# Batched 64x64 matmul on one core: stores in 1 KB runs, output copied out by half partitions, and transposes of bf16 pairs

## The chip, the cores and the metric

The kernel runs on one core of one Trainium2 chip. The metric is the device time of one execution in microseconds (us). Runs are compared by their median; a profile shows one execution, with its own time.

## The reference

```python
def setup_inputs():
    return {
        "a": np.random.randn(1024, 64, 64).astype(np.float32),
        "b": np.random.randn(1024, 64, 64).astype(np.float32),
    }

def reference(a, b):
    return np.matmul(a, b).astype(np.float32)
```

There are 1024 independent products of 64x64 matrices. Each of a, b and the result holds 16.78 MB in fp32, so 33.55 MB are read and 16.78 MB written.

## The kernel before

**Tiles.** b and the result go in 16 tiles t of 64 batches (1 MB each), a in 8 tiles s of 128 batches (2 MB each), so one a tile serves two tiles t. A batch in a tile t is g*4 + h, with 16 groups g of four batches h. Four batches share one matmul: their 64 values of k are taken as 32 pairs (k = 2*kp + u), the contraction runs over the 128 partitions (h kp), and the two values of u are summed in PSUM. The stationary operand is block diagonal: rows of batch h meet only the 32 columns of batch h, and the rest stays at the zeros that two memsets put there at the start.

**The steps for a.** `load_a(s)` (L60) issues four DMAs of 512 KB on the POOL queue, one for each h, in runs of 4 KB, and casts to bf16 on the way. `regroup(s)` (L85) is one VectorE copy that puts the four h side by side, `a_bf`. `transpose(s, w)` (L92) makes 16 TensorE transposes of 128x128 bf16 (every second k, `u::2`, of one row of a per partition) into two PSUM tiles `at_ps`; VectorE copies one to `at_sb` and ScalarE the other, both with a reordering of the free dimensions. It is called for w = 0 and w = 1, so 32 transposes for an a tile. `spread(t)` (L107) is four VectorE copies inside SBUF, one for each h, of 32 partitions x 2048 bf16 elements: they put `at_sb` into the diagonal blocks of one of two tiles `at_bd`.

**The steps for b and the result.** `load_b(t)` (L70) is one DMA of 1 MB in runs of 512 B (two rows of k in one partition), on ScalarE's queue for t = 1 and 3 and on SyncE's (SP) queue otherwise. `cast(t)` (L117) is one ScalarE copy to bf16, or four quarters over both engines for the last tile. `multiply(t)` (L135) makes 64 pairs of weight load and matmul (16 g x 2 w x 2 u, 64 columns each) into four PSUM tiles `o_ps` of one bank, each of which ScalarE copies, 128 partitions x 512 elements, to `o_sb` (for the last tile, VectorE takes every second one). `store(t)` (L131) issues the DMA of 1 MB from `o_sb` on the POOL queue, in runs of 512 B: a partition (h mo) holds two rows of the result, w = 0 and 1, for each g. The last tile's store is issued in four quarters.

**Buffers.** Three a tiles, four b tiles, two each of `a_bf`, `at_sb`, `b_bf` and `at_bd`, five `o_sb`; in PSUM four `at_ps` and four `o_ps`, one bank each.

**The order.** It is written by hand (`tc.manual_schedule()`): each engine and each DMA queue takes its instructions in the order of the program text. For each t the text has `spread(t+1)`; for even t then `regroup(s+2)` and `load_a(s+4)`; `multiply(t)`; `cast(t+1)`; `load_b(t+4)`; a half of the transposes of a coming a tile; and `store(t-1)`. At the start `load_a(0)` comes first; the memset of the identity matrix stands behind its first DMA, and b(0) and b(1) carry an added dependency on that memset:

```python
            if s == 0 and h == 1:
                begun.append(nc.gpsimd.memset(identity[:], 0.0))
...
                reason="first load of a goes ahead",
```

Of the kernel before, what the change touches and what calls it, by code (L numbers as in the profile page):

```python
# [6 lines left out]

fp32 = mybir.dt.float32
bf16 = mybir.dt.bfloat16
# [3 lines left out]
def kernel(  # L13
# [9 lines left out]

    nc = tc.nc
    B, M, K = a.shape
    _, _, N = b.shape
# [2 lines left out]
    n_t, n_s = B // 64, B // 128  # L31
    A_AHEAD = 3
    B_AHEAD = 4
    N_BD = 2
# [1 line left out]

    a_v = a.rearrange("(s g h) (mp v) k -> s h g mp (v k)", h=4, g=32, v=16)
    b_v = b.rearrange("(t g h) (kp u) n -> t (h kp) g (u n)", h=4, g=16, u=2)
    o_v = out.rearrange("(t g h) (mo w) n -> t (h mo) g (w n)", h=4, g=16, w=2)

    consts = ctx.enter_context(tc.tile_pool(name="consts", bufs=1))
    a_pool = ctx.enter_context(tc.tile_pool(name="a_pool", bufs=A_AHEAD))
    b_pool = ctx.enter_context(tc.tile_pool(name="b_pool", bufs=B_AHEAD))
    work = ctx.enter_context(tc.tile_pool(name="work", bufs=2))
    o_pool = ctx.enter_context(tc.tile_pool(name="o_pool", bufs=5))
    t_psum = ctx.enter_context(
        tc.tile_pool(name="t_psum", bufs=4, space=bass.MemoryType.PSUM)
    )
    o_psum = ctx.enter_context(
        tc.tile_pool(name="o_psum", bufs=4, space=bass.MemoryType.PSUM)  # L50
    )

    bd_tiles = [
        consts.tile([128, 64, 4, 32], bf16, name=f"at_bd{i}") for i in range(N_BD)
    ]
    identity = consts.tile([128, 128], bf16)
    a_tiles, b_tiles, abf_tiles, at_tiles, bbf_tiles = {}, {}, {}, {}, {}
    held, begun = {}, []

    def load_a(s):  # L60
        a_sb = a_pool.tile([128, 4, 16, 64], bf16, name="a_sb")
        for h in range(4):
            if s == 0 and h == 1:
                begun.append(nc.gpsimd.memset(identity[:], 0.0))  # L64
            nc.gpsimd.dma_start(  # L65
                out=a_sb[:, h, :, :].rearrange("p v k -> p (v k)"), in_=a_v[s, h]
            )
        a_tiles[s] = a_sb

    def load_b(t):  # L70
        b_sb = b_pool.tile([128, 16, 128], fp32, name="b_sb")
        queue = nc.scalar if t in (1, 3) else nc.sync
        load = queue.dma_start(out=b_sb[:], in_=b_v[t])  # L73
        if t < 2:
            tc.add_manual_dep(
                load.ins,
                begun[0].ins.name,
                mybir.DependencyInfo(
                    mybir.DependencyClass.Sync, mybir.DependencyReason.DATA
                ),  # L80
                reason="first load of a goes ahead",
            )
        b_tiles[t] = b_sb

    def regroup(s):  # L85
        a_sb = a_tiles.pop(s)
        a_bf = work.tile([128, 16, 4, 64], bf16, name="a_bf")
        nc.vector.tensor_copy(a_bf[:], a_sb[:].rearrange("p h v k -> p v h k"))  # L88
        abf_tiles[s] = a_bf
        at_tiles[s] = work.tile([128, 2, 2, 128, 8], bf16, name="at_sb")  # L90

    def transpose(s, w):  # L92
        a_cols = abf_tiles[s][:].rearrange("p v h k -> p v (h k)")
        for u in range(2):
            at_ps = t_psum.tile([128, 8, 128], bf16, name="at_ps")
            for vo in range(8):
                nc.tensor.transpose(  # L97
                    at_ps[:, vo, :], a_cols[:, 2 * vo + w, u::2], identity[:]
                )
            dst = at_tiles[s][:, w, u, :, :]  # L100
            src = at_ps[:].rearrange("p vo q -> p q vo")
            if u == 0:
                nc.vector.tensor_copy(dst, src)  # L103
            else:
                nc.scalar.copy(dst, src)  # L105

    def spread(t):  # L107
        at_v = at_tiles[t // 2][:].rearrange(
            "p w u (g mp) vo -> p (w u) g (mp vo)", g=32
        )  # L110
        half = slice(16 * (t % 2), 16 * (t % 2) + 16)
        bd_v = bd_tiles[t % N_BD][:].rearrange("p (wu g) h mo -> p wu g h mo", g=16)
        for h in range(4):
            rows = slice(32 * h, 32 * h + 32)
            nc.vector.tensor_copy(bd_v[rows, :, :, h, :], at_v[rows, :, half, :])  # L115

    def cast(t):  # L117
        b_bf = work.tile([128, 16, 128], bf16, name="b_bf")
        b_sb = b_tiles.pop(t)
        if t < n_t - 1:  # L120
            nc.scalar.copy(b_bf[:], b_sb[:])  # L121
        else:
            for gq in range(4):
                rows = slice(4 * gq, 4 * gq + 4)
                if gq % 2:
                    nc.vector.tensor_copy(b_bf[:, rows, :], b_sb[:, rows, :])  # L126
                else:
                    nc.scalar.copy(b_bf[:, rows, :], b_sb[:, rows, :])  # L128
        bbf_tiles[t] = b_bf

    def store(t):  # L131
        for piece in held.pop(t):
            piece()

    def multiply(t):  # L135
        at_bd, b_bf = bd_tiles[t % N_BD], bbf_tiles.pop(t)
        last = t == n_t - 1
        o_sb = o_pool.tile([128, 4, 4, 2, 64], fp32, name="o_sb")

        def put(gq):  # L140
            nc.gpsimd.dma_start(  # L141
                out=o_v[t, :, 4 * gq : 4 * gq + 4, :],
                in_=o_sb[:, gq, :, :, :].rearrange("p g w n -> p (g w n)"),
            )

        def put_all():
            nc.gpsimd.dma_start(  # L147
                out=o_v[t], in_=o_sb[:].rearrange("p q g w n -> p (q g w n)")
            )

        for gq in range(4):
            o_ps = o_psum.tile([128, 4, 2, 64], fp32, name="o_ps")
            for g4 in range(4):
                g = 4 * gq + g4
                for w in range(2):
                    for u in range(2):
                        nc.tensor.matmul(  # L157
                            o_ps[:, g4, w, :],
                            at_bd[:, (2 * w + u) * 16 + g, :, :].rearrange(
                                "p h mo -> p (h mo)"  # L160
                            ),
                            b_bf[:, g, 64 * u : 64 * u + 64],
                            start=(u == 0),
                            stop=(u == 1),
                        )
            if last and gq % 2:
                nc.vector.tensor_copy(o_sb[:, gq, :, :, :], o_ps[:])  # L167
            else:
                nc.scalar.copy(o_sb[:, gq, :, :, :], o_ps[:])  # L169
        held[t] = [lambda q=q: put(q) for q in range(4)] if last else [put_all]  # L170

    with tc.manual_schedule():
        load_a(0)
        for t in range(B_AHEAD):
            load_b(t)
        for bd in bd_tiles:
            nc.vector.memset(bd[:], 0.0)  # L177
        nc.gpsimd.affine_select(  # L178
            out=identity[:],
            in_=identity[:],  # L180
            compare_op=mybir.AluOpType.not_equal,
            fill=1.0,
            base=0,
            pattern=[[-1, 128]],
            channel_multiplier=1,
        )
        for s in range(1, A_AHEAD):
            load_a(s)
        regroup(0)
        transpose(0, 0)  # L190
        transpose(0, 1)
        spread(0)
        cast(0)
        regroup(1)
        load_a(A_AHEAD)
        transpose(1, 0)
        for t in range(n_t):
            s, half = t // 2, t % 2
            if t + 1 < n_t:
                spread(t + 1)  # L200
            if half == 0:
                if s + 2 < n_s:
                    regroup(s + 2)
                if s + 1 + A_AHEAD < n_s:
                    load_a(s + 1 + A_AHEAD)
            multiply(t)
            if t + 1 < n_t:
                cast(t + 1)
            if t + B_AHEAD < n_t:
                load_b(t + B_AHEAD)  # L210
            if half == 0 and s + 1 < n_s:
                transpose(s + 1, 1)
            if half == 1 and s + 2 < n_s:
                transpose(s + 2, 0)
            if t >= HOLD - 1:
                store(t - HOLD + 1)
        for t in range(n_t - HOLD + 1, n_t):
            store(t)
# [30 lines left out]
```

## Time and profile before

| what | value |
|---|---|
| median of 5 runs (lowest to highest) | 139.31 us (138.28 to 139.67) |
| profiled execution, its own time | 139.6 us |
| its span (first to last instruction) | 137.7 us |
| HBM traffic over the span | 365 GB/s |
| busy: VectorE (DVE) | 84.9 us, 62% |
| busy: ScalarE (ACT) | 77.4 us, 56% |
| busy: TensorE matmul (PE), weight load (PEld) | 58.5 us, 56.5 us |
| busy: GpSimd (POOL), DMA issue included | 42.3 us, 31% |
| DMA queue 0 (POOL: a and the result), share of 16 engines | 66.2% |
| DMA queues 1 and 10 (SP and ScalarE: b), share of 16 engines | 30.1%, 3.9% |

How to read it: the span is what the profile covers, and the execution's time has 1.9 us around it. Engines run side by side, so busy times don't add up to the span. The 16 DMA engines serve all queues; their row in the profile's slices gives their mean busy share in tenths of a slice of 3.4 us, and the GB/s beside it counts the bytes written, so a cast from fp32 to bf16 counts half of what it reads. A group of instructions is one line of the kernel on one engine: its busy time, the mean time of one, and the idle time of the engine just ahead of them with what ended it. L12 is line 12 of the kernel before.

### The profile page before, as it was taken

To read this page: it belongs to the slowest core of one execution; us is meant where nothing else is said; L and a number is where in the kernel's file an instruction comes from. 1 tells how busy PE (TensorE), PEld (TensorE's weight loads), DVE (VectorE), ACT (ScalarE), POOL (GpSimd) and SP (SyncE) were. 2 spreads that over 40 slices of the span, in tenths; PEclk is the share of its full clock that TensorE was granted. 3 is DMA by queue.
4 is the path that set the end of the run, shared out by engine and by line. 5 is a ranking of instruction groups with operands and counts; after the bars stand their busy time and mean duration, and the time that the engine had idled before them with its cause. 6 is when DMAs were issued, how large, how long until landed. Compare 5 with 4: busy or idle time off the path is not lost.

```text
span 137.7 us, 2995 instructions
## 1 busy us (share of the span) xinstructions
PE 58.5 (42%) x1280; PEld 56.5 (41%) x1280; DVE 84.9 (62%) x94; ACT 77.4 (56%) x98; POOL 42.3 (31%) x57
## 2 busy tenths in 40 slices
PE   0000720595349745862065800857019645507100
PEld 0000720595249744761065800856019645507100
DVE  5771574681999899999339850699207867904200
ACT  0103171099917999960789209791297999715100
POOL 6921411332731612333113443430030330232600
PEclk9999996589965899999559995599955999995955
DMA  2999999999999999999999999999999999999980
GB/s 28 181 300 306 305 305 308 299 271 259 233 272 270 339 338 271 281 372 386 314 272 299 380 378 296 272 323 385 374 381 382 377 384 384 377 383 375 301 255 21
DMA packets 17469, 42.14 MB, mean 306 GB/s; under 512 B 1072, under 2 KB 1072, under 8 KB 17456
## 3 DMA queue, kind: packets, MB, share of 16 engines
q0 software_dynamic: 9008, 25.17, 66.2%
q1 hardware_dynamic: 7392, 14.68, 30.1%
q10 hardware_dynamic: 1056, 2.10, 3.9%
q8 instruction: 10, 0.16, 0.4%
q14 instruction: 3, 0.02, 0.0%
HBM read 33.55 MB, written 16.78 MB: 365 GB/s over the span
## 4 chain that ended last, share of the span: by engine, by line
DMA 57%; issue 25%; POOL 11%; POOLq 1%
DMA a_sb<-in_a_dram 40%; DMA out_dram<-o_sb 18%; POOL out_dram L147 6%; POOL a_sb L65 3%; POOL out_dram L141 2%; POOLq L244 1%; POOL identity L178 0%; POOL identity L64 0%; POOLq L147 0%; POOLq L178 0%; POOLq L141 0%; POOLq L65 0%; POOLq L233 0%
## 5 line engine op out<-in xcount | busy, mean ns | idle before, releaser
L157 PE MATMUL o_ps<-b_bf,at_bd 128*128 128x64 bf16 x1024 | 40.2, 208 | 46.7 <-ACT b_bf L121 38.8
L115 DVE COPY at_bd<-at_sb 32x2048 bf16<-32x2048 bf16 x64 | 46.9, 732 | 21.4 <-ACT at_sb L105 20.4
L157 PEld LDWEIGHTS <-at_bd 128*128 128x128 bf16 x1024 | 39.6, 108 | 48.2 <-issue 36.1
L169 ACT COPY o_sb<-o_ps 128x512 f32<-128x512 f32 x62 | 33.5, 615 | 25.8 <-DMA out_dram<-o_sb 17.0
L65 POOL DMA_DIRECT2D a_sb<-in_a_dram x32 | 20.1, 642 | 41.3 <-DMA a_sb<-in_a_dram 30.7
L147 POOL DMA_DIRECT2D out_dram<-o_sb x15 | 18.6, 1237 | 41.7 <-ACT o_sb L169 26.7
L97 PE MATMUL at_ps<-identity,a_bf 128*128 128x128 bf16 x256 | 20.5, 245 | 22.8 <-DVE a_bf L88 22.8
L121 ACT CAST b_bf<-b_sb 128x2048 bf16<-128x2048 f32 x15 | 29.1, 1943 | 0.0
L97 PEld LDWEIGHTS <-a_bf 128*128 128x128 bf16 x256 | 18.0, 112 | 23.2 <-DVE a_bf L88 23.2
L105 ACT COPY at_sb<-at_ps 128x1024 bf16<-128x1024 bf16 x16 | 16.8, 1048 | 11.7 <-PE at_ps L97 11.7
L103 DVE COPY at_sb<-at_ps 128x1024 bf16<-128x1024 bf16 x16 | 19.5, 1221 | 3.8 <-PE at_ps L97 3.5
L88 DVE COPY a_bf<-a_sb 128x4096 bf16<-128x4096 bf16 x8 | 10.0, 1250 | 10.2 <-DMA a_sb<-in_a_dram 10.1
L177 DVE MEMSET at_bd<- 128x4096 uint32 x2 | 6.9, 3472 | 2.5 <-PEq L233 1.7
L105 ACT ACT_TABLE_LOAD x1 | 1.3, 1283 | 6.9 <-issue 6.9
L141 POOL DMA_DIRECT2D out_dram<-o_sb x4 | 3.0, 754 | 4.4 <-ACT o_sb L169 4.1
L167 DVE COPY o_sb<-o_ps 128x512 f32<-128x512 f32 x2 | 1.4, 690 | 2.6 <-PE o_ps L157 2.6
L128 ACT CAST b_bf<-b_sb 128x512 bf16<-128x512 f32 x2 | 1.1, 616 | 3.1 <-DMA b_sb<-in_b_dram 3.1
L126 DVE CAST b_bf<-b_sb 128x512 bf16<-128x512 f32 x2 | 0.8, 424 | 3.4 <-DMA b_sb<-in_b_dram 3.4
L73 ACT MOVE_SHAPE b_sb<-in_b_dram x2 | 0.6, 320 | 3.2 <-POOL identity L64 2.2
L178 POOL TENSOR_SCALAR_AFFINE_SELECT identity<-identity 128x128 bf16<-128x128 bf16 x1 | 0.4, 354 | 0.0
L64 POOL MEMSET identity<- 128x128 bf16 x1 | 0.2, 224 | 0.0
L233 POOL MEMSET const-float32-0.0<- 128x1 f32 x1 | 0.1, 99 | 0.2 <-issue 0.2
(3 smaller groups left out, 0.3 us busy)
## 6 DMA issues: line engine op xcount, KB each, us to landing
out_dram<-o_sb POOLq DMA_DIRECT2D x15, 1024.0 KB, 21.2
a_sb<-in_a_dram POOLq DMA_DIRECT2D x32, 256.0 KB, 18.0
out_dram<-o_sb POOLq DMA_DIRECT2D x4, 256.0 KB, 7.6
b_sb<-in_b_dram SPq DMA_DIRECT2D x14, 0.5 KB, 21.1
b_sb<-in_b_dram ACTq DMA_DIRECT2D x2, 0.5 KB, 22.0
```

The source lines that it names most:

```text
L65: nc.gpsimd.dma_start(out=a_sb[:, h, :, :].rearrange("p v k -> p (v k)"), in_=a_v[s, h])
L88: nc.vector.tensor_copy(a_bf[:], a_sb[:].rearrange("p h v k -> p v h k"))
L97: nc.tensor.transpose(at_ps[:, vo, :], a_cols[:, 2 * vo + w, u::2], identity[:])
L103: nc.vector.tensor_copy(dst, src)
L105: nc.scalar.copy(dst, src)
L115: nc.vector.tensor_copy(bd_v[rows, :, :, h, :], at_v[rows, :, half, :])
L121: nc.scalar.copy(b_bf[:], b_sb[:])
L141: nc.gpsimd.dma_start(out=o_v[t, :, 4 * gq : 4 * gq + 4, :], in_=o_sb[:, gq, :, :, :].rearrange("p g w n -> p (g w n)"),)
L147: nc.gpsimd.dma_start(out=o_v[t], in_=o_sb[:].rearrange("p q g w n -> p (q g w n)"))
L157: nc.tensor.matmul(o_ps[:, g4, w, :], at_bd[:, (2 * w + u) * 16 + g, :, :].rearrange("p h mo -> p (h mo)"), b_bf[:, g, 64 * u : 64 * u + 6 ...
L169: nc.scalar.copy(o_sb[:, gq, :, :, :], o_ps[:])
L177: nc.vector.memset(bd[:], 0.0)
```

## The change

- The result goes out in runs of 1 KB. The view of the output puts four consecutive rows into one partition (x mo), where x counts eight batches and mo sixteen groups of four rows; the DMAs are as many and as large as before.
- To have four rows in a partition, an output tile in PSUM now holds two of them (j) in its free dimension and two (wl) in the two halves of its partitions. `evacuate` copies each half of the partitions, for each parity of g, to the place it belongs to: four copies of 64 partitions x 512 elements for half a tile t. The first half of a tile goes to ScalarE, the second to VectorE; for the last tile it goes by quarters, with eight copies of 64 x 256 elements on each engine. There are two `o_ps` tiles of two banks each, where there were four of one bank.
- A transpose takes a pair of bf16 values (u = 0 and 1) as one 4 byte element, so an a tile has 16 transposes of 128x128 fp32 elements instead of 32 of bf16. All copies of `at_ps` to `at_sb` are ScalarE's, 128 partitions x 512 fp32 elements. `spread` moves 1024 fp32 elements for each partition in place of 2048 bf16 ones. The matmul reads its weights from `at_bd` as bf16 with a step of two elements; matmuls are as many as before, and of the same size.
- `cast(t+1)` and `load_b(t+4)` stand between the two halves of `multiply(t)`.
- The identity is fp32 and is made by `make_identity` after the loads of a(0) and the first four loads of b are issued; the added dependency of b(0) and b(1) is gone.

The diff, cut to its core:

```diff
-    o_v = out.rearrange("(t g h) (mo w) n -> t (h mo) g (w n)", h=4, g=16, w=2)
+    o_v = out.rearrange("(t gh x) (mo w) n -> t (x mo) gh (w n)", gh=8, x=8, w=4)
...
-        tc.tile_pool(name="o_psum", bufs=4, space=bass.MemoryType.PSUM)
+        tc.tile_pool(name="o_psum", bufs=2, space=bass.MemoryType.PSUM)
...
-        consts.tile([128, 64, 4, 32], bf16, name=f"at_bd{i}") for i in range(N_BD)
+        consts.tile([128, 2, 16, 2, 4, 16], fp32, name=f"at_bd{i}") for i in range(N_BD)
...
-    identity = consts.tile([128, 128], bf16)
+    identity = consts.tile([128, 128], fp32)
...
-            if s == 0 and h == 1:
-                begun.append(nc.gpsimd.memset(identity[:], 0.0))
...
-        load = queue.dma_start(out=b_sb[:], in_=b_v[t])
-        if t < 2:
-            tc.add_manual_dep(
...
+        queue.dma_start(out=b_sb[:], in_=b_v[t])
...
-        at_tiles[s] = work.tile([128, 2, 2, 128, 8], bf16, name="at_sb")
-
-    def transpose(s, w):
-        a_cols = abf_tiles[s][:].rearrange("p v h k -> p v (h k)")
-        for u in range(2):
-            at_ps = t_psum.tile([128, 8, 128], bf16, name="at_ps")
-            for vo in range(8):
+        at_tiles[s] = work.tile([128, 2, 32, 2, 4, 4], fp32, name="at_sb")
+
+    def transpose(s, j):
+        a_cols = abf_tiles[s][:].rearrange("p v h k -> p v (h k)").bitcast(fp32)
+        for wl in range(2):
+            at_ps = t_psum.tile([128, 4, 128], fp32, name="at_ps")
+            for vo in range(4):
                 nc.tensor.transpose(
-                    at_ps[:, vo, :], a_cols[:, 2 * vo + w, u::2], identity[:]
+                    at_ps[:, vo, :], a_cols[:, 4 * vo + 2 * j + wl, :], identity[:]
                 )
-            dst = at_tiles[s][:, w, u, :, :]
-            src = at_ps[:].rearrange("p vo q -> p q vo")
-            if u == 0:
-                nc.vector.tensor_copy(dst, src)
-            else:
-                nc.scalar.copy(dst, src)
+            nc.scalar.copy(
+                at_tiles[s][:, j, :, wl, :, :],
+                at_ps[:].rearrange("p vo (g mp) -> p g mp vo", mp=4),
+            )
...
-            nc.vector.tensor_copy(bd_v[rows, :, :, h, :], at_v[rows, :, half, :])
+            nc.vector.tensor_copy(
+                bd[rows, :, :, :, h, :].rearrange("p j g wl mo -> p j (g wl) mo"),
+                at_tiles[t // 2][rows, :, half, :, :, :].rearrange(
+                    "p j g wl mp vo -> p j (g wl) (mp vo)"
+                ),
+            )
...
+        at_bd = bd_tiles[t % N_BD][:].rearrange("p j g wl h mo -> p j g (wl h mo)")
+        at_bd = at_bd.bitcast(bf16).rearrange("p j g (c u) -> p j g c u", u=2)
...
+        def evacuate(o_ps, gh, gl, n, copy):
+
+            for par in range(2):
+                for wl in range(2):
+                    src = o_ps[64 * wl : 64 * wl + 64, gl : gl + n, par, :, :]
+                    dst = o_sb[64 * par : 64 * par + 64, gh : gh + n, :, wl, :]
+                    copy(dst, src)
+
+        for half in range(2):
+            o_ps = o_psum.tile([128, 4, 2, 2, 64], fp32, name="o_ps")
+            for g8 in range(8):
+                g = 8 * half + g8
+                for j in range(2):
                     for u in range(2):
                         nc.tensor.matmul(
...
+                            o_ps[:, g8 // 2, g8 % 2, j, :],
+                            at_bd[:, j, g, :, u],
                             b_bf[:, g, 64 * u : 64 * u + 64],
...
+                if last and g8 % 4 == 3:
+                    gl = g8 // 4 * 2
+                    copy = nc.vector.tensor_copy if gl else nc.scalar.copy
+                    evacuate(o_ps, 4 * half + gl, gl, 2, copy)
+            if not last:
+                copy = nc.vector.tensor_copy if half else nc.scalar.copy
+                evacuate(o_ps, 4 * half, 0, 4, copy)
+            if half == 0:
+                between()
...
+    def advance(t):
+        if t + 1 < n_t:
+            cast(t + 1)
+        if t + B_AHEAD < n_t:
+            load_b(t + B_AHEAD)
...
-        nc.gpsimd.affine_select(
-            out=identity[:],
...
+        make_identity(nc, identity)
...
-            multiply(t)
-            if t + 1 < n_t:
-                cast(t + 1)
-            if t + B_AHEAD < n_t:
-                load_b(t + B_AHEAD)
+            multiply(t, lambda: advance(t))
```

## The prediction

> **What bounds the kernel now.** I read the forty slices first, because an average over the span would mix stages.
>
> ```profile
> PE   0000720595349745862065800857019645507100
> DVE  5771574681999899999339850699207867904200
> ACT  0103171099917999960789209791297999715100
> DMA  2999999999999999999999999999999999999980
> GB/s 28 181 300 306 305 305 308 299 271 259 233 272 270 339 338 271 281 372 386 314 272 299 380 378 296 272 323 385 374 381 382 377 384 384 377 383 375 301 255 21
> ```
>
> The DMA row stands at 9 from the second slice to the 38th; every other engine has slices at 0 to 3. So the 16 DMA engines are the bound from about 3 us to 134 us, about 131 us or 8.2 us for each of the 16 tiles, and what an engine gains or loses counts only if the DMA engines are left without work. GB/s counts what is written, and a is cast on the way (4 bytes read, 2 written), so low figures mean "a in flight", not "slow". Then four stretches of the trace by time (columns: stretch, busy us and count by engine, PE clock, DMA share, GB/s):
>
> ```profile
> 4.00:6.50 2.50, 0.00 (x0) 0.00 (x0) 1.70 (x2) 0.00 (x0) 2.50 (x6) 1.00 1.09 195
> 6.90:20.00 13.10, 3.59 (x32) 3.33 (x32) 6.87 (x5) 4.03 (x4) 3.31 (x5) 1.00 1.08 304
> 97.00:125.00 28.00, 12.12 (x295) 11.82 (x295) 14.88 (x21) 21.27 (x29) 5.84 (x5) 0.86 1.03 381
> 128.50:133.50 5.00, 0.00 (x0) 0.00 (x0) 0.21 (x1) 0.00 (x0) 1.32 (x2) 0.75 0.97 280
> ```
>
> In order: almost only a, in 4 KB runs, 195 written and so 390 read; a and b together; b loads and stores, both in 512 B runs, 381; stores alone at the end, 280. The DMA share is full in all of them, so these are rates of the engines, not lack of work. Next, what the rest of the kernel waits for (waiter, what for: us in total, times, longest):
>
> ```profile
> DVE at_bd L115 <- ACT at_sb L105: 20.4, 6, 6.6
> ACT o_sb L169 <- DMA out_dram<-o_sb: 17.0, 3, 5.9
> ```
>
> Three times for some 5.5 us ScalarE waits for a store to free one of the five o_sb buffers, and VectorE waits behind it: the arithmetic runs ahead of the DMA by five tiles. That is the cover for added work. Last, the groups whose durations I use (busy us, mean ns):
>
> ```profile
> L157 PE MATMUL o_ps<-b_bf,at_bd 128*128 128x64 bf16 x1024 | 40.2, 208 | 46.7 <-ACT b_bf L121 38.8
> L115 DVE COPY at_bd<-at_sb 32x2048 bf16<-32x2048 bf16 x64 | 46.9, 732 | 21.4 <-ACT at_sb L105 20.4
> L169 ACT COPY o_sb<-o_ps 128x512 f32<-128x512 f32 x62 | 33.5, 615 | 25.8 <-DMA out_dram<-o_sb 17.0
> L105 ACT COPY at_sb<-at_ps 128x1024 bf16<-128x1024 bf16 x16 | 16.8, 1048 | 11.7 <-PE at_ps L97 11.7
> L103 DVE COPY at_sb<-at_ps 128x1024 bf16<-128x1024 bf16 x16 | 19.5, 1221 | 3.8 <-PE at_ps L97 3.5
> L167 DVE COPY o_sb<-o_ps 128x512 f32<-128x512 f32 x2 | 1.4, 690 | 2.6 <-PE o_ps L157 2.6
> ```
>
> **What the Trainium skill says.** (1) DMA: Bandwidth & Descriptors, "Why small descriptors are slow": about 3 cycles of fixed cost beside one cycle per 32 B. This gives 19 cycles for 512 B and 35 for 1 KB, so 38 against 35 for the same bytes, 8% less. The trace agrees in direction only: 390 read at 4 KB against 381 at 512 B, where casting and direction differ too. (2) VectorE: DVE Perf Modes, "The perf-mode tier table": a copy inside SBUF runs at 4 elements a cycle in bf16 and at 2 in fp32. The first half agrees: 2048 elements in 732 ns. The second is not in this trace. (3) TensorE: Matmul & The Clock Gate, "Terms" names a transpose mode, "4× faster for FP32"; no fp32 transpose is in this trace.
>
> **The change, part by part.** The sum is made against the profiled execution, 139.6 us (span 137.7 and 1.9 around it); the median of the five times is 139.31, 0.3 lower.
>
> Stores: 16.78 MB leave in 1 KB runs instead of 512 B. At 381 GB/s they take 44.0 us of the DMA's time. The 8% gives 3.5 us as an estimate from the skill; if runs of 1 KB only reach the 390 of the 4 KB reads, 1.0; nothing, if half the traffic beside them (b, still in 512 B runs) sets the pace; and if the 280 of stores alone shows what 512 B writes cost by themselves, up to 5. I take 2.5. The POOL queue issues the same 51 transfers; its 1 MB issues (about 1.2 us each, against 0.75 for a quarter) should shorten, which is worth nothing as POOL is 31% busy.
>
> Start: b(0) and b(1) no longer wait for the memset that stands behind the first piece of a. ScalarE waits 2.2 us for it now, and the DMA engines are only filled at 4.0 us. Filled 1 us earlier, all that follows comes 1 us earlier: I take 1.0 (0 to 1.5). The price is that b shares the engines while a(0) has them alone: half of 195 GB/s over 2.5 us is 0.24 MB, which a gets back at one piece of 0.26 MB per 2.4 us, so a(0) lands up to 2.2 us later. The identity's two instructions on POOL now follow all four pieces of a(0), under 2 us later, long before the first transpose at 14.6. All that delays compute, not the DMA: three a and four b buffers hold 10.5 MB of HBM reads, 26 us at 400 GB/s.
>
> VectorE: removed, 16 copies of at_ps (19.5 us busy) and two of o_ps (1.4). Added, 4 half-partition copies for each of 15 tiles and 8 of half the length for the last: half the partitions save no time, the elements per partition count, so 60 x 690 ns = 41.4 and 8 x 420 = 3.4. The spread moves 1024 fp32 elements instead of 2048 bf16 ones: at half the rate the same cycles, 732 ns; at one element a cycle it would be near the 1221 of L103 (1024 elements). I take 732. The engine goes from 84.9 to 84.9 - 20.9 + 44.8 = 109 us. Per tile 4 x 0.73 + 4 x 0.69 + half a regroup (0.63) = 6.3 us, now 4.8; under the DMA's 8.2, so it is hidden by the DMA. What queues behind the new copies on VectorE, which wait for the second half of a multiplication, are the next spread and regroup; the spread of the next tile stands ahead of them, so TensorE has one tile in hand.
>
> ScalarE: 16 copies of 1048 ns become 32 of 128x512, 615 ns, and its part of o_ps stays at four copies a tile: +3 us, per tile 1.94 + 4 x 0.54 + 2 x 0.6 = 5.3 us, hidden likewise. The cast of the next b and its load's issue move between the two halves of the multiplication; on ScalarE they stand behind the same four copies as before, so SP's loads go out at the same point.
>
> TensorE: 256 transposes become 128 of 4 byte elements. Sixteen take 1.06 us now (66 ns each); eight at that price 0.5 us a tile, at four passes 2.1. Weights read with a step of two elements: the transposes do so now, inside those 66 ns, where a matmul pair takes 2.03 us/64 = 32 ns; so 2.0 to 4.2 us a tile. At worst 6.3 us a tile, still under 8.2. Only two halves of o_ps exist instead of four quarters; the second half waits for VectorE's 2.8 us of the tile before.
>
> End: the last b lands at 124.0 us and about 3 MB of stores are still to go, so the DMA has 9 us of work while the last tile is computed. That tile's last copies are four of 420 ns instead of one of 690: 1.0 us later, and up to 1.7 more if strided weights are slow. I charge 0.5, because store backlog covers most (0 to 2).
>
> Sum: -2.5 - 1.0 + 0.5 = -3.0: 136.6 for the profiled execution, 136.3 against the median.
>
> **The rivals.** *Dearer writes:* stores alone at 280 GB/s are far under the 381 of the mixture; if that is the cost of 512 B writes, the gain is 5 and the end speeds up too: 133.8. Against it: with b beside them the same stores reach 381. *Run length does not matter:* 390 and 381 are nearly equal; then only the start (-1.0) is left against the end and a later first tile (+1.0): 139.3. *The start costs more than it gives:* a(0) 2.2 us late, then sixteen fp32 transposes in front of the first tile at four passes and cold clock (3.6 us now, up to 7), so VectorE starts its 96 us of work after the first multiplication (27.3 now) near 31 and ends at 127 only if it never idles. It decides once VectorE idles over some 3 us after that. One wait of the longest kind shown above, 6.6 us, puts its end at 133.6, 4.9 later than the 128.7 of now; less 1.0 for the earlier fill and 2.5 for the stores, 139.3 becomes 140.7. *The spread loses its fast mode:* 64 x 1.2 = 77 us instead of 47, VectorE 139 us, 8.2 a tile, at the DMA's own pace; with the 11 us it idles before its first spread and 8 after the last store's issue, 158 us. It decides from about 1.2 us per spread. Against it: the present one is in its fast mode with the same shape of runs (64 B).
>
> **How the numbers follow.** A difference under 0.5% (0.7 us) could not be told from none here. Forecast 0.60, around 136.3 with an own range of 134.5 to 138.0; dearer writes 0.13; no effect 0.10; slow start 0.10; slow spread 0.07. Faster 0.73, same 0.10, slower 0.17. The range of 133.0 to 140.0 leaves out the slow spread, most of the slow start and the far end of dearer writes, together under 0.2.
>
> **What would show it.** Right: the DMA row still at 9 throughout, GB/s near 400 in the stretches that now show 381, and above 280 at the end; the DMA filled before 4 us; the spread at about 0.73 us; VectorE near 109 us; waits of o_sb for stores still there. Wrong: slices of DMA under 9 in the middle; the spread at 1.1 us or more; stores and b at 381 as before; a regroup of a(0) after 16 us with the rest shifted alike.

## The result, and the profile after

The changed kernel takes 139.06 us (median; 138.5 to 139.4), the kernel before, measured beside it, 139.01 us (138.07 to 140.28). The ratio is 1.0001 with a 95% interval of 0.9987 to 1.0015: no difference, where 136.3 us had been forecast. The profiled span went from 137.7 to 137.3 us.

From the profile's page of the changed kernel, the rows of the forty slices (3.43 us each):

```profile
DVE  5770124968699999999999999999999999979440
DMA  2999999999999999999999999999999999993493
GB/s 86 310 300 310 302 278 254 209 255 273 232 253 306 380 278 267 360 395 353 276 273 388 399 316 267 308 398 393 396 396 399 387 391 395 380 357 138 167 327 122
```

Three things are to be seen. The second slice has 310 GB/s where it had 181, but the row of the DMA is at 9 there in both: before, it was a that was loaded then, which counts half. How much more the DMA works at the start is in its share from 2 to 4 us, in the kernel before and then in the changed one (columns as in the prediction):

```profile
2.00:4.00 2.00, 0.00 (x0) 0.00 (x0) 2.00 (x1) 0.64 (x2) 1.96 (x5) 1.00 0.65 69
2.00:4.00 2.00, 0.00 (x0) 0.00 (x0) 2.00 (x1) 0.29 (x1) 1.93 (x5) 1.00 0.79 246
```

That is 0.3 us of work. In the stretch of b and stores the DMA moves 387 to 399 where it moved 374 to 385. But its row now has a hole, 3 and 4 in the 37th and 38th slices (138 and 167 GB/s), just before the end, and VectorE's row is at 9 without a break for 24 slices, to 120 us. Four stretches of the changed kernel's trace:

```profile
4.00:6.50 2.50, 0.00 (x0) 0.00 (x0) 1.70 (x2) 0.08 (x1) 2.32 (x5) 1.00 1.07 302
97.00:125.00 28.00, 15.45 (x288) 14.80 (x289) 26.21 (x38) 21.01 (x29) 4.86 (x4) 0.68 1.01 384
125.00:130.00 5.00, 1.88 (x33) 1.77 (x33) 3.41 (x7) 2.91 (x8) 1.93 (x3) 0.50 0.27 91
128.50:133.50 5.00, 1.01 (x16) 0.85 (x15) 2.54 (x6) 1.40 (x4) 2.19 (x4) 0.50 0.94 314
```

and the third of them in the kernel before:

```profile
125.00:130.00 5.00, 2.99 (x61) 2.86 (x58) 1.38 (x2) 1.32 (x3) 3.01 (x4) 0.75 1.02 335
```

The DMA share in 125 to 130 us falls from 1.02 to 0.27, and the data moved from 335 to 91 GB/s. (TensorE's granted clock is lower too: 0.50 for 0.75, and 0.68 for 0.86 in 97 to 125 us.) With 1 KB runs, stores alone then go at 314 instead of 280. The wait of ScalarE for a store to free an `o_sb` buffer, 17.0 us in three stretches before, is nearly gone, and POOL now waits for VectorE with its stores (the changed kernel's waits):

```profile
POOL out_dram L135 <- DVE o_sb L146: 33.3, 9, 5.8
ACT o_sb L146 <- DMA out_dram<-o_sb: 2.0, 1, 2.0
```

So the arithmetic no longer runs ahead until all five `o_sb` buffers are full. The groups:

```profile
L102 DVE COPY at_bd<-at_sb 32x1024 f32<-32x1024 f32 x64 | 47.3, 739 | 7.2 <-ACT at_sb L92 5.3
L146 DVE COPY o_sb<-o_ps 64x512 f32<-64x512 f32 (+1 forms) x68 | 44.7, 657 | 4.2 <-PE o_ps L154 2.2
```

The spread at 739 ns and the half copies are as priced; VectorE is busy for 109.4 us (109 forecast), ScalarE for 87.2 (some 80 forecast, counted up from 77.4; its groups added up to 82.4 us before, so that 5 us of them overlapped, and to 87.3 now, hardly overlapping).

What happens around the hole is in the timelines of TensorE (the first line, tile 14) and VectorE (start, us, operation, then the idle time before it and what ended it):

```profile
118.98 3.57 PE L154 MATMUL o_ps<-b_bf,at_bd 128*128 128x64 bf16 x64 [4.19 <-ACT b_bf L113]
119.14 3.09 DVE L102 COPY at_bd<-at_sb 32x1024 f32<-32x1024 f32 x4
123.18 0.76 DVE L118 CAST b_bf<-b_sb 128x512 bf16<-128x512 f32 x2 [0.95 <-DMA b_sb<-in_b_dram]
123.95 2.79 DVE L146 COPY o_sb<-o_ps 64x512 f32<-64x512 f32 x4
127.63 1.73 DVE L146 COPY o_sb<-o_ps 64x256 f32<-64x256 f32 x4 [0.89 <-issue]
131.10 1.73 DVE L146 COPY o_sb<-o_ps 64x256 f32<-64x256 f32 x4 [1.74 <-PE o_ps L154]
```

and in POOL's, which issues the stores:

```profile
127.30 1.59 POOL L135 DMA_DIRECT2D out_dram<-o_sb  x2 [6.28 <-ACT o_sb L146]
129.66 1.43 POOL L135 DMA_DIRECT2D out_dram<-o_sb  x2 [0.78 <-DVE o_sb L146]
133.12 0.72 POOL L135 DMA_DIRECT2D out_dram<-o_sb  x1 [2.04 <-DVE o_sb L146]
```

The last b lands at 123.2 us, and its cast, which the change put between the two halves of tile 14, stands ahead of the four copies of tile 14's second half on VectorE. TensorE had these products ready at 122.55, but the copies begin at 123.95, so store(14) goes out at 127.30. In the kernel before it went out six microseconds earlier:

```profile
121.34 1.15 POOL L147 DMA_DIRECT2D out_dram<-o_sb  x1 [3.34 <-ACT o_sb L169]
```

By GB/s times length, 2.7 MB (tiles 14, 15 and part of 13) were left to move when the last b landed at 123.2, where the kernel before had 3.25 MB left at 124.0. But only some 0.6 MB of the 2.7 stood in the queue, since neither tile 14 nor 15 was out; before, all but tile 15 did, some 2.2 MB. At 384 GB/s the 0.55 MB are 1.4 us, so the DMA was 0.8 + 1.4 = 2.2 us ahead at that point, by this estimate. Behind it, the 2.7 MB at 330 GB/s (the rate of the stores from 130 to 134) would take 8.2 us; DMA share 0.63 over the 12.5 us from 123.2 to 135.7 says that it worked for some 8 and idled for the rest. In the kernel before, the same stretch has a share of 0.87. The DMA's lead was given back there.

### The profile page after: what moved, and what is told of

Its sections match the earlier page's. It is cut to its first block, busy times and chain, and to the rows that moved or that the text cites. A ratio compares the mean times of both kernels' runs of the same rounds, so it can differ in the third digit from the quotient of the medians.

```text
span 137.3 us, 2820 instructions
## 1 busy us (share of the span) xinstructions
PE 67.0 (49%) x1152; PEld 63.1 (46%) x1152; DVE 109.4 (80%) x144; ACT 87.2 (64%) x120; POOL 40.8 (30%) x57
## 4 chain that ended last, share of the span: by engine, by line
DMA 49%; SPq 17%; issue 11%; PE 7%; DVE 5%; ACT 5%; POOL 3%; POOLq 1%; DVEq 0%; ACTq 0%
DMA a_sb<-in_a_dram 32%; SPq L74 17%; DMA b_sb<-in_b_dram 17%; PE at_ps L89 4%; PE o_ps L154 3%; ACT b_bf L113 3%; DVE o_sb L146 2%; DVE a_bf L80 2%; POOL out_dram L135 2%; ACT o_sb L146 1%; DVE at_bd L102 1%; POOL a_sb L66 1%; POOLq L241 1%; ACT at_sb L92 0%; DVEq L80 0%
## 5 line engine op out<-in xcount | busy, mean ns | idle before, releaser
L154 PE MATMUL o_ps<-b_bf,at_bd 128*128 128x64 bf16 x1024 | 45.9, 214 | 40.9 <-ACT b_bf L113 14.5
L154 PEld LDWEIGHTS <-at_bd 128*128 128x128 bf16 x1024 | 43.7, 112 | 44.4 <-issue 20.3
L102 DVE COPY at_bd<-at_sb 32x1024 f32<-32x1024 f32 x64 | 47.3, 739 | 7.2 <-ACT at_sb L92 5.3
L146 DVE COPY o_sb<-o_ps 64x512 f32<-64x512 f32 (+1 forms) x68 | 44.7, 657 | 4.2 <-PE o_ps L154 2.2
L146 ACT COPY o_sb<-o_ps 64x512 f32<-64x512 f32 (+1 forms) x68 | 37.8, 555 | 13.7 <-PE o_ps L154 10.6
L135 POOL DMA_DIRECT2D out_dram<-o_sb x19 | 20.6, 1087 | 66.2 <-DVE o_sb L146 33.3
L89 PE MATMUL at_ps<-identity,a_bf 128*128 128x128 f32 x128 | 24.5, 357 | 23.1 <-DVE a_bf L80 23.1
L92 ACT COPY at_sb<-at_ps 128x512 f32<-128x512 f32 x32 | 18.0, 588 | 20.9 <-PE at_ps L89 20.5
L89 PEld LDWEIGHTS at_ps<-identity,a_bf 128*128 128x128 f32 x128 | 20.4, 188 | 23.3 <-issue 23.3
L186 DVE MEMSET at_bd<- 128x4096 f32 x2 | 6.9, 3472 | 2.5 <-PEq L230 1.7
```

The costliest lines, as they stand in the source:

```text
L89: nc.tensor.transpose(at_ps[:, vo, :], a_cols[:, 4 * vo + 2 * j + wl, :], identity[:])
L92: nc.scalar.copy(at_tiles[s][:, j, :, wl, :, :], at_ps[:].rearrange("p vo (g mp) -> p g mp vo", mp=4),)
L102: nc.vector.tensor_copy(bd[rows, :, :, :, h, :].rearrange("p j g wl mo -> p j (g wl) mo"), at_tiles[t // 2][rows, :, half, :, :, :].rearrange(
L135: nc.gpsimd.dma_start(out=o_v[t, :, lo : lo + n, :], in_=o_sb[:, lo : lo + n].rearrange("p gh j wl n -> p (gh j wl n)"),)
L154: nc.tensor.matmul(o_ps[:, g8 // 2, g8 % 2, j, :], at_bd[:, j, g, :, u], b_bf[:, g, 64 * u : 64 * u + 64], start=(u == 0), stop=(u == 1),)
```

## The experiments

Each run is given by its median and by its ratio to the kernel before measured beside it, with the 95% interval in brackets; the diffs of e1 to e7, e10 to e16 and e18 are against the changed kernel unless another is named. The theory at the start: VectorE has become the bound, and the transfers that were to cover the last tile are gone by then.

**Is VectorE the bound?** Two kernels move or add its work.

e4: VectorE repeats one half copy in 15 tiles.

```diff
+                if half:
+                    copy(o_sb[64:128, 4:8, :, 1, :], o_ps[64:128, 0:4, 1, :, :])
```

> VectorE repeats one of its half-partition copies in each of 15 tiles (10.5 us more work for it, same result). Theory V: nearly all of it shows, 8 to 10.5 us, about 148. Rival D: the DMA hides it as far as VectorE has slack, under 2 us.

149.01 us, ratio 1.0718 [1.0672, 1.0765]; the changed kernel took 139.06, so 10.4 us of copies cost 9.9. Above its present work VectorE has almost no slack, while the forecast gave it 1.9 us a tile.

e1: one in four of VectorE's half copies goes to ScalarE.

```diff
-                    copy(dst, src)
+                    (fourth if fourth and par and wl else copy)(dst, src)
```

> One of VectorE's four half-partition copies per tile goes to ScalarE (15 of 60, about 10.5 us off VectorE and 8.3 on ScalarE). Theory V (after the change VectorE's unbroken row of work from 22 to 127 us sets the end): 3 to 5 us faster than the changed kernel, near 134 to 136, until the DMA is the bound again. Rival D (the DMA is still the bound and 1 KB runs gave nothing): within 0.5 us of 139.

141.06 us, ratio 1.0139 [1.0099, 1.0179], though VectorE was busy for 97.0 us only. The copy on ScalarE waits for VectorE's copies into the same part of `o_sb`, as the waits of e1 show (8.8 us, 12 times), and ScalarE is then late for its next cast:

```profile
ACT o_sb L146 <- DVE o_sb L146: 8.8, 12, 1.3
```

Less work on the bound engine was paid for with a wait between two engines. It did not test the theory, so two further kernels lighten VectorE in other ways. e12: in odd tiles ScalarE takes the two copies into the other half of the partitions.

```diff
+                help_dve = half == 1 and t % 2 == 1
+                evacuate(
+                    o_ps, 4 * half, 0, 4, copy, nc.scalar.copy if help_dve else None
+                )
```

> In each second tile ScalarE takes two of VectorE's four half-partition copies, those that write the other half of the partitions of o_sb, so that neither engine waits for the other's writes (7 tiles, 9.8 us off VectorE, 8.3 us on ScalarE; per tile 5.9 us on both). Theory V: 2 to 4 us faster than the changed kernel. Theory W (both engines' chains are at their limit, as in the first attempt at balance, where ScalarE had a cycle of 6.5 us): no gain, or 1 to 2 us slower.

139.14 us, ratio 1.0011 [0.9986, 1.0036].

e10: the spread of the fourth h is left out.

```diff
-        for h in range(4):
+        for h in range(3):
```

> The changed kernel with the spread of the fourth batch of each group left out (its products come out as zeros): 16 x 0.73 = 11.7 us less for VectorE and nothing added to another engine. Theory V (VectorE's row from the third regroup at 30 us to the copy of tile 14 at 126.7 us decides when the last two stores can start): the 4 us in which the DMA stood idle at the end vanish and the time falls by 3 to 4 us, to 135 to 136, where the DMA is the bound. Rival W (any engine's lag would show: ScalarE or TensorE is as late as VectorE): less than 1 us.

139.63 us, ratio 1.004 [1.0017, 1.0064], with VectorE at 97.1 us. So 12 us less on VectorE bring nothing, where 10.4 more cost nearly all of themselves. e10's timelines of ScalarE and of VectorE, one line each, show what holds instead:

```profile
116.70 1.90 ACT L113 CAST b_bf<-b_sb 128x2048 bf16<-128x2048 f32 x1 [1.58 <-DMA b_sb<-in_b_dram]
```

```profile
123.41 0.76 DVE L118 CAST b_bf<-b_sb 128x512 bf16<-128x512 f32 x2 [3.01 <-DMA b_sb<-in_b_dram]
```

VectorE now stands idle for 3.01 us until the last b lands, at 123.41 instead of 123.18. The copies of tile 14's second half wait behind the cast of that b, though TensorE had finished at 122.22, and store(14) goes out at 127.53: the rest of the chain is as it was. Two limits of equal height meet there: VectorE's row of work and the landing of the last b. The first theory is half the truth.

Why the last b hardly lands earlier with faster stores is in the packets of each queue, from 97 to 115 us in the kernel before (q0 is POOL's queue, here with stores alone, q1 SP's with b; packets, MB, share of the 16 engines):

```profile
q0 software_dynamic: 1173, 4.54, 67.4%
q1 hardware_dynamic: 1170, 2.31, 35.0%
```

While both queues have work they send packet for packet, and a packet of stores holds twice as much, some 4 KB to 2. So a tile of stores leaves in 4.2 us and a tile of b arrives in 8.2; e10 still has 1214 packets of stores to 1217 of b. The faster stores speed up both queues by the same few per cent. In the changed kernel the stores' queue runs short from 112 to 118 us (324 packets to 552 of b), and there VectorE's pace shows; but b fills the gap, and DMA time is lost only once b has landed.

**The start.** e8 is the kernel before without the dependency of b(0) and b(1).

```diff
-        if t < 2:
-            tc.add_manual_dep(
...
-                reason="first load of a goes ahead",
```

> The kernel before with only the added dependency of b(0) and b(1) taken off. If the earlier filling of the DMA engines is worth 1.0 us in a kernel that the DMA bounds: 138. If a(0) coming later costs as much: 139, no difference.

138.63 us, ratio 0.9968 [0.9946, 0.999]: the early start alone is worth 0.4 us, with the regroup of a(0) at 16.88 instead of 13.36. e2 puts the dependency back into the changed kernel.

```diff
+            if s == 0 and h == 1:
+                begun.append(nc.gpsimd.memset(identity[:], 0.0))
...
+        if t < 2:
+            tc.add_manual_dep(
```

> b(0) and b(1) wait again for the memset behind the first piece of a, as before the change. Theory V with a late start: the first regroup comes back from 16.8 to about 13.5 us, VectorE's row starts 2 to 3 us earlier and the end comes 1.5 to 3 us earlier, about 136 to 137.5. Rival D: the DMA fills 1.5 us later, so 1 us slower, about 140.

140.78 us, ratio 1.0119 [1.007, 1.0169]. The regroup of a(0) is back at 12.85, but VectorE waits for a(2):

```profile
32.81 1.23 DVE L91 COPY a_bf<-a_sb 128x4096 bf16<-128x4096 bf16 x1 [5.04 <-DMA a_sb<-in_a_dram]
34.05 2.08 DVE L157 COPY o_sb<-o_ps 64x512 f32<-64x512 f32 x3
```

Its first copy of the output starts at 34.05, where the changed kernel has 31.96, and the kernel ends 1.7 us later. At the end the casts of b(15) no longer wait for its load (VectorE's, at 124.81, comes straight after other work). So here it is VectorE's unbroken row that sets the end, and the early filling is worth more in the changed kernel than before because this row begins with it.

**The run length.** e3 stores the changed kernel's tiles as two DMAs with runs of 512 B.

```diff
+            for j in range(2):
+                nc.gpsimd.dma_start(
+                    out=o_v[t, :, lo : lo + n, 128 * j : 128 * j + 128],
```

> Each store leaves as two transfers with runs of 512 B instead of one with 1 KB, all else as in the changed kernel. Theory V: the DMA has about 4 us of unused time at the end of the changed kernel, so losing 3 to 4 us of store rate costs little, 0 to 2 us. Rival D with a real gain from 1 KB: 3 to 4 us slower. Rival D without: the same. The rate where b and stores run alone tells the gain itself: 396 GB/s with 1 KB, near 381 if the run length made the difference.

142.67 us, ratio 1.0262 [1.022, 1.0303]. b and stores together fall to 375 to 385 GB/s. The issues doubled too (ten of them at the end took 7.4 us of POOL), so e3 alone does not price the run length. Two kernels without arithmetic do: e5 loads a and b and stores zeros in 1 KB runs, e6 in 512 B runs.

```diff
-    o_v = out.rearrange("(t gh x) (mo w) n -> t (x mo) gh (w n)", gh=8, x=8, w=4)
+    o_v = out.rearrange("(t g h) (mo w) n -> t (h mo) g (w n)", h=4, g=16, w=2)
```

> All arithmetic is left out: the same loads of a and b and the same 1 MB stores in 1 KB runs, from a fixed tile of zeros, on the same queues. Theory: what remains is the DMA's own time, 126 to 130 us. Its difference from the 512 B twin is what the run length is worth: 3.5 us by the price that the prediction used (2.5 was taken).

> The twin of the run before with stores in 512 B runs, in the layout of the kernel before; arithmetic left out as well. If run length is worth what was predicted, 2.5 to 3.5 us more than the 1 KB twin; if it is worth nothing, the same.

e5 takes 135.03 us, ratio 0.9727 [0.9695, 0.9759]; e6 142.32, ratio 1.0253 [1.0219, 1.0286]: 7.3 us for the run length. Nearly all of it lies where stores have the engines alone. The stretch from 121 to 129 us of e5, then of e6 (the columns now begin with VectorE, ScalarE and POOL):

```profile
121.00:129.00 8.00, 0.00 (x0) 0.00 (x0) 0.00 (x0) 1.00 1.01 350
```

```profile
121.00:129.00 8.00, 0.00 (x0) 0.00 (x0) 0.00 (x0) 1.00 1.00 268
```

So 512 B writes by themselves cost 1.3 times as much for the same bytes as 1 KB writes (350 / 268), while beside b's reads the two mixtures differ by some 4% (387 to 399 against 374 to 385). The bytes of the changed kernel, with nothing to wait for, need 135.0 us. That is no floor for the kernel: e6, without arithmetic, is slower than the whole kernel before, since its stores run alone for longer. The twins price writes alone; they don't show that 4 us could be had.

**The tail.** The second theory: what sets the end is the chain from the last b through cast, multiplies and copies to the last store. e7 gives each quarter of the last tile a PSUM tile of its own, so that the second half does not wait for the copies of the first.

```diff
+                if last and g8 % 4 == 0:
+                    bank = t_psum.tile([128, 4, 128], fp32, name="at_ps")
```

> The changed kernel with a PSUM tile of its own for each quarter of the last output tile, so that the next quarter's matmuls don't wait for the copies of the quarter before. Theory T (these waits, 1.6 us twice, lengthen the exposed end): 2.5 to 3.5 us faster, about 136. Rival (the stores behind set the end): no difference.

139.19 us, ratio 1.0025 [1.0005, 1.0045]. VectorE's last copy ends at 130.3 instead of 132.8, yet store(14) still goes out at 127.30 and the hole in the DMA's row remains. From there the 2.1 MB of tiles 14 and 15 need 6.4 us at 330 GB/s, however early the last tile is copied: the late store(14) sets the end. e11 stores tiles 12 to 14 in halves:

```diff
+        elif t >= n_t - 4:
+            held[t] = [lambda: put(0, 4), lambda: put(4, 4)]
```

> The stores of tiles 12 to 14 are issued in two halves, so that ScalarE's half of tile 14, ready at 123.2 us, need not wait for VectorE's, ready at 126.7. Theory V: half a MB moves into the idle 4 us of the DMA, 1.3 to 1.6 us faster than the changed kernel, about 137.5. If the end is not set by when these stores start: no difference.

140.38 us, ratio 1.0088 [1.0054, 1.0123]; the last issue came at 134.39 instead of 133.12. A miss, and its trace shows where: b(15) was cast at 124.47 instead of 123.18, and all behind it is as much later. e13 is e12, e11 and e7 together.

> The last two edits together, with a PSUM tile for each quarter of the last output tile. Theory V: the gains add until the DMA bounds, about 135 to 136, faster than both kernels. If the balance does not work: as with halves alone, 137.5.

138.53 us, ratio 0.997 [0.9951, 0.9989]: 0.4 us faster than before. The last b lands at 124.5 in it, and the DMA is idle at 127 to 130 (share 0.23 in 126 to 128 and 0.14 in the next 2 us). e18 adds to e13 that b(15) is loaded in four quarters of 256 KB, each cast just before its multiplies, so that the cast no longer stands ahead of tile 14's copies:

```diff
+        if t == n_t - 1:
+            for q in range(4):
+                rows = slice(4 * q, 4 * q + 4)
+                queue.dma_start(out=b_sb[:, rows, :], in_=b_v[t, :, rows, :])
...
+                    late[0](2 * half + g8 // 4)
```

> The kernel e13 (evacuations balanced in odd tiles, last stores in halves, last quarters in PSUM tiles of their own) with b(15) loaded in four quarters of 512 KB and each quarter cast just before the multiplies that use it, so that the last cast no longer stands on VectorE ahead of tile 14's copies. Theory (the latency chain from the landing of the last b to the last store sets the end, while the DMA idles): 2 to 3.5 us below e13, that is 135 to 136.5 us. Rival (the DMA's total work sets the end whatever the order): 138.5 us as e13.

137.86 us, ratio 0.9917 [0.9889, 0.9945]: the fastest kernel of this study, 1.2 us below before and 0.7 below e13 by the ratios, where 2 to 3.5 were expected. Tile 14's second half now goes out at 125.84, where e13 has 128.41. The DMA's hole is filled in part; two stretches of e18:

```profile
126.00:128.00 2.00, 1.68 (x30) 1.56 (x30) 0.87 (x4) 1.25 (x3) 1.30 (x2) 0.50 0.69 242
128.00:130.00 2.00, 0.99 (x20) 0.88 (x18) 1.25 (x3) 1.47 (x4) 0.72 (x1) 0.50 0.73 252
```

But the chain itself is no shorter. VectorE's timeline of e18 ends

```profile
128.87 0.43 DVE L123 CAST b_bf<-b_sb 128x512 bf16<-128x512 f32 x1
130.40 1.73 DVE L153 COPY o_sb<-at_ps 64x256 f32<-64x256 f32 x4 [1.10 <-PE at_ps L168]
```

at 132.13, against 131.64 in e13: cast, multiplies (1.01 us for 16 pairs at a granted clock of 0.50) and copies of a quarter follow each other, and casting waits for the copies on the same engine. The theory holds in direction; its size was too large, because only the order of the chain was changed and not its work. TensorE's clock is a part of that work which no run sets apart: the 64 pairs of tile 14 take 3.57 us in the changed kernel and in e18, where the kernel before took 2.03.

e19 does the same quarters of b(15) in the kernel before, where queued stores should cover the chain.

> The kernel before with b(15) loaded and cast in four quarters in the same way. Theory: no gain (within 0.5 us of before), since in the kernel before some 3 MB of stores are queued when the last b lands and cover the chain behind it. Rival (the chain behind the last b sets the end in both kernels): 1.5 us or more below before.

143.03 us, ratio 1.0313 [1.0267, 1.0358]. It does not test the theory, since the quarters landed far later than the whole b(15) did (124.0):

```profile
134.14 0.43 DVE L131 CAST b_bf<-b_sb 128x512 bf16<-128x512 f32 x1 [2.79 <-DMA b_sb<-in_b_dram]
```

The packets of e19 from 115 to 121 us show why:

```profile
q0 software_dynamic: 511, 1.97, 88.8%
q1 hardware_dynamic: 512, 0.25, 14.2%
```

The queues still send packet for packet, but a packet of a quarter of b(15) holds only 0.5 KB, so b comes at 42 GB/s as long as stores are queued. In e18 fewer were: 241 packets beside 1320 of b from 119 to 123 us.

**An earlier last b.** b could be brought forward at the cost of the stores. e14 puts b(11), b(13) and b(15) on ScalarE's queue, so that b has two queues beside the one of the stores.

```diff
-        queue = nc.scalar if t in (1, 3) else nc.sync
+        queue = nc.scalar if t in (1, 3, 11, 13, 15) else nc.sync
```

> The changed kernel with b(11), b(13) and b(15) issued on ScalarE's queue instead of SP's, so that b has two queues against the one of the stores at the end. Theory L (two limits of equal height: the last b lands at 123 to 124 us because b gets half of the DMA's rate, however fast the stores are, AND VectorE's row ends at 126.7): b(15) lands well before 120, but VectorE's row still ends near 126 and the time moves by less than 1 us. Theory L without VectorE (the last b alone): 2 to 4 us faster.

141.52 us, ratio 1.0197 [1.0171, 1.0223]. e15 is e14 without the fourth h's spread, e16 is e13 with the two queues, e17 the kernel before with them.

> The same with the spread of the fourth batch of each group left out (its products are zeros), which alone had given nothing. Theory L with both limits: now both are gone, 3 to 5 us faster than the changed kernel, 134 to 136. Theory W (neither matters, the DMA's own work is the bound): still 139.

> The two queues for b with ScalarE's help in each second tile, stores of tiles 12 to 14 in halves and a PSUM tile for each quarter of the last tile; nothing left out. Theory L: the real form of the run before, 135 to 137, clearly faster than both kernels. Theory W: 138.5, as without the second queue.

> The kernel before with the same three loads of b on ScalarE's queue. Theory L: the kernel before keeps 3 MB of stores for the time after its last b, so an earlier b only lengthens the part in which stores run alone at 280 GB/s: no gain, between 0 and 2 us slower. If the last b alone decided everywhere: 2 to 3 us faster.

140.91 us, ratio 1.0144 [1.0107, 1.018]; 138.37, ratio 0.9977 [0.9957, 0.9998]; 142.16, ratio 1.0232 [1.0205, 1.0259]. The expectation of e14 gives b half of the rate; by the packets it had a third, and two queues for b mean two packets of b for one of stores (295, 297 and 299 from 97 to 103 us in e14). So b came earlier (in e15 nothing waits for it any longer), but the stores slowed, the five `o_sb` buffers filled, and ScalarE had to wait for them in the middle. From the waits of e15:

```profile
ACT o_sb L146 <- DMA out_dram<-o_sb: 12.6, 2, 7.4
```

Then e17 ends with stores alone, at 250 to 290 GB/s for four slices. Bringing b forward moves the wait from the last b to the buffers. e15 lightened VectorE as well and was to reach 134 to 136: moving both limits brought up a third.

## Why the prediction was wrong, point by point

- **Stores, -2.5.** Right in kind. Beside b the mixture gains 4%; since stores are two thirds of its bytes, that is some 5% of their own cost (an estimate), near the 2.5 us of 44. Alone they go from 268 to 350 in the twins, 280 to 314 in the kernels themselves. The 8% estimated from the fixed cost in the Trainium skill (DMA: Bandwidth & Descriptors, "Why small descriptors are slow") lies between these two. The rival of dearer writes read the 280 correctly. POOL's issues hardly shortened: a 1 MB store issue takes 0.9 to 1.4 us.
- **Start, -1.0: mis-sized.** The DMA was filled earlier as foreseen, but the time up to 4.0 us was not empty before: its share from 2 to 4 us was 0.65 and is now 0.79, 0.3 us of work. a(0) came 3.4 us later (16.80 instead of 13.36), where up to 2.2 were priced; e8 puts the net at -0.4.
- **Stores and start together** were to save 3.5 us of the DMA's time; 2.2 of that were there when the last b landed, by the estimate above.
- **End, +0.5: the step that failed.** "The DMA has 9 us of work while the last tile is computed" was read from the kernel before and carried over. That work has to be stores already in the queue, and at the landing of the last b there were 0.6 MB of them instead of 2.2. The prediction followed the moved cast on ScalarE alone, but half of the cast of b(15) is VectorE's: it stands ahead of tile 14's copies, so store(14) came at 127.30 instead of 121.34, and 125 to 130 us had a DMA share of 0.27 instead of 1.02. About 2 us of DMA lead were lost there, against the 0.5 charged. e7 shows that the last tile's own copies (1.73 us for the four of a quarter, about as priced) and the waits of 1.59 us between its quarters are not what cost; e18, which brings tile 14's copies forward again, is with its other edits 1.2 us faster.
- **VectorE hidden: wrong as well, but not decisive alone.** The sizes were right: 109.4 us for 109; 6.5 us a tile for 6.3 while a is regrouped (eight tiles from 46.12 to 98.47 us), and 5.95 without. The comparison was wrong: 8.2 us is the DMA's pace averaged over the span, a included. Once a is in, a tile of stores leaves in 4.2 us, so a lead of finished tiles is worked off in the last 28 us, and little of it is left as cover. e4 shows the missing slack. But e10 takes 12 us off VectorE and gains nothing.
- **Not seen at all: the last b.** It lands at 123 to 124.5 us in the kernels before, after, e10 and e13, since b's queue gets a packet for each packet of stores and so a third of the rate. This is why a lighter VectorE (e10, e12) gains nothing by itself.
- **The rivals.** The spread kept its fast mode: 739 ns, as the skill's two fp32 elements a cycle (VectorE: DVE Perf Modes, "The perf-mode tier table") would have it. The slow start had the right mechanism, an unbroken VectorE row that begins near 31 and ends at 126.7; its price of 6.6 us for another long wait never fell due. "Run length does not matter" names the measured time (139.3) by luck: the trace has stores alone at 314 for 280 GB/s and b with stores 4% faster.
- **TensorE.** Eight fp32 transposes take 1.07 us at full clock, 134 ns each against 66: the same per byte, twice the low price taken and half of the high one. Strided weights cost nothing (below).

## What to carry to other kernels

Compare an engine's time per tile with the bound's pace in the stage where the two run side by side, not with its mean over the span, and take the pace of each queue apart: here stores left twice as fast as b arrived, and a lead of several buffers was used up by the end. Work that queued transfers cover stays covered only as long as the transfers are still queued, so a faster DMA must be followed to the last load: ask what stands in the queue when it lands, and how long the chain behind it is. Follow a moved instruction on every engine that it runs on, the last tile's special case included. Where two limits are of equal height, lightening one shows nothing, and moving both can bring up a third.

## What the runs showed of the hardware

- Writes by themselves depend on the run length far more than writes beside reads: 268 and 350 GB/s for 512 B and 1 KB alone (e6, e5), some 380 and 393, reads included, with b's reads in 512 B runs beside them.
- Queues that all have work send packet for packet (1173 to 1170; 511 to 512; 299 to 295 and 297), and the packets differ in size: some 4 KB for the stores, 2 KB for a whole tile of b, 0.5 KB for a quarter of one. So the rate of a load depends on what it shares the engines with: 128 GB/s for whole tiles and 42 for quarters beside the same stores. A third queue shifts service from the stores to b (e14 to e17).
- A weight load of bf16 with a step of two elements is as fast as one without. From the changed kernel's timeline of TensorE, 64 pairs in 2.03 us (32 ns a pair, as before), and eight fp32 transposes:

```profile
34.66 2.03 PE L154 MATMUL o_ps<-b_bf,at_bd 128*128 128x64 bf16 x64 [1.83 <-ACT b_bf L113]
75.50 1.07 PE L89 MATMUL at_ps<-identity,a_bf 128*128 128x128 f32 x8
```
